# The state update in three split passes, the 31-tap convolution's sum in a PSUM bank, and three banks for small products

## The chip, the core and the metric

The kernel is one layer of a decoder trunk in fp32. It runs on one core of a Trainium2 chip: TensorE (PE) for matmuls, VectorE (DVE), ScalarE (ACT) and GpSimd (POOL) for everything else, SyncE (SP) for most transfers. The metric is the device time of one execution in microseconds (us), the median of several runs; lower is better.

## The reference

The layer mixes the positions of a sequence of 1024 rows with 1024 channels by two gated branches, projects the mix, and adds a gated feed-forward network with a small convolution. The parts that the change touches are the 31-tap convolution of the first branch and the chunked recurrence of the second:

```python
def conformer_branch(u_glu, dw_w, dw_b, ln_g, ln_b, w_out):
    a, g = jnp.split(u_glu, 2, axis=-1)
    v = a * jax.nn.sigmoid(g)
    v = causal_dwconv(v, dw_w, dw_b)             # 31 taps for each channel
    v = jax.nn.silu(layer_norm(v, ln_g, ln_b))
    return v @ w_out
# ssd_chunked, for chunks of 128 positions
    y_diag = jnp.einsum("bcgrls,bcsgrp->bclgrp", cb[:, :, :, None] * decay, xs)
    states = jnp.einsum("bclgn,bcgrl,bclgrp->bcgrpn", bc, decay_states, xs)
    # prev: the state carried into each chunk, decayed and added up
    y_off = jnp.einsum("bclgn,bcgrpn,bcgrl->bclgrp", cc, prev, jnp.exp(a_cs))
# the layer
    y_a = conformer_branch(u_glu, ...)
    y_b = ssd_branch(z, xbc, dt_raw, ...)
    mix = (jax.nn.sigmoid(gate_a) * y_a + jax.nn.sigmoid(gate_b) * y_b) @ w_o[l]
    h = layer_norm(DN_ALPHA * h + mix, ln1_g[l], ln1_b[l])
    h = layer_norm(DN_ALPHA * h + conv_ffn(h, ...), ln2_g[l], ln2_b[l])
```

## The kernel before

**Precision.** The large products keep fp32's accuracy by splitting each operand into a high part, rounded to the type fp32r, and a low part, the rest; `mm3` (L190 to L192) then makes three fp32r passes, high by high, high by low and low by high, in one accumulation. A weight block of 1024 rows and 128 columns is loaded, cast on ACT (L156), and its low part taken on DVE (L161); `project` runs eight such triples, 24 passes of 128x512, for one block of 128 output channels by 512 positions. Small products (transposes, the masks, the recurrence's own) are plain fp32 matmuls. In the profile one fp32 matmul shows as two instructions at L661, L808 and L820 (x56 there for 28 products).

**Stages.** The sequence is worked through in two halves of 512 positions (hh = 0, 1). For each half: `mixers`, then `combine`, then the output projection `out_proj` for hh = 0; the feed-forward part for both halves stands at the end, behind `mixers(1)` and `combine(1)`. In `mixers` four groups g follow each other. A group projects its columns (B, C, four of x, four of z, and two pairs for the convolution), convolves some with 4 taps (`conv4`, L517), gates the pairs (`glu`) into two tiles v, runs the recurrence (`ssd_group`) on four chunks of 128 positions, and the 31-tap convolution (`conv31`) on its two v. At the end come the first half of the recurrence branch's output projection and some gates.

**A chunk of the recurrence.** PE transposes four blocks of x into one PSUM bank (px, L614), and B of the chunk with the product of B and C into another (pb, L617 and L618). DVE makes xs and xsd from px (xs with the time step; xsd, L643, with the decay to the chunk's end), ACT copies the transposed B to bt, and DVE multiplies the decay mask m by the product (L648). Then PE forms the output py from m and xs (L653) and from the carried state and ce (L656), and the state's increment pn in one fp32 matmul of bt and xsd (L661). DVE decays the state (L665), adds pn (L668), and reads py in four skip additions (L671). `last` leaves the increment out in each group's last chunk of the second half: 28 increments in all.

**The 31-tap convolution.** For each v, ACT makes the first term with the bias in the accumulator c, and DVE adds thirty taps (L564, `scalar_tensor_tensor`, c = v shifted by k, times a column of weights, plus c). The two tiles of a group alternate, so each tap stands behind one of the other chain. Eight channel blocks c0_0 to c0_7 (c1_... in the second half), 480 taps in all. The sums of the first six blocks go to memory and come back later; the last two stay. The convolution has a low priority (offset -1500), so its taps fill DVE's gaps.

**Combine.** For the convolution branch's norm, POOL adds the eight blocks (L801, L803), PE takes the mean over channels with a matmul on a constant (L808, `deviations`), DVE subtracts it (L810), ACT squares (L812, L815), POOL adds the squares (L816, seven additions), PE takes the mean again (L820, `normed`), ACT the root (L821), DVE the reciprocal (L822), and for each block DVE multiplies (L825), ACT applies silu (L826), casts (L206), and DVE takes the low part (L207): that is sT, which the products with `wconv` (weights w_co) read. Around it PE has the products of the second gate (weights w_gb) and of the recurrence branch's second half (w_sp); DVE adds and multiplies their results into mb (L861, L862).

**Banks.** PSUM has eight banks: four (`pacc`, tiles acc) for the large products, and four (`psm`, tiles sm) through which all small products rotate.

**Order.** The program is recorded once; a scheduler, with priorities from the order of the code and the offsets given in it, lays the instructions out, engine by engine, and each engine works its own list strictly in that order. A tile that reuses a buffer waits for the readers of its former user.

Of the kernel before, what the change touches and what calls it, by code (L numbers as in the profile page):

```python
# [16 lines left out]
P = 128  # L17
# [6 lines left out]
KC = 31  # L24
# [37 lines left out]
def kernel(  # L62
# [28 lines left out]
    psm = ctx.enter_context(tc.tile_pool(name="psm", bufs=4, space=PSUM))  # L91
# [3 lines left out]
    def bank(which):  # L95
        n_ps[0] += 1
        pl, tag = (pacc, "acc") if which else (psm, "sm")
        return pl.tile([P, 512], F32, tag=tag, name=f"{tag}{n_ps[0]}")
# [187 lines left out]
    def ln_in_first():  # L286
        hT = big_tile("hT0")
        with pool("lnin0", side="right") as pl:
# [11 lines left out]
            for pair in range(2):  # L300
                with tc.high_priority(offset=3500 if pair else 6000):
                    pts = [bank(0).rearrange("p (k t) -> p k t", k=2) for _ in range(4)]
# [227 lines left out]
    def glu(pl, hh, hT, i):  # L530
        pa, pg = bank(1), bank(1)
        wa = col_weights(hh, CT_A + i)
        project(pa, wa, hT)
        wg = col_weights(hh, CT_G + i)
        project(pg, wg, hT)
        v = (statep if i & 2 else pl).tile(
            [P, HALF + KC - 1], F32, tag="v", bufs=2, name=f"v{hh}_{i}"
        )
        s = pl.tile([P, HALF], F32, tag="sig", name=f"sig{hh}_{i}")
        A.activation(out=s, in_=pg, func=AF.Sigmoid)  # L540
        A.copy(v[:, : KC - 1], v_halo[:, i, :])
        V.tensor_mul(v[:, KC - 1 :], pa, s)
        if hh == 0:
            A.copy(v_halo[:, i, :], v[:, HALF:])
        return v

    def conv31(pl, hh, vs):

        accs = {}
        for i, v in vs:  # L550
# [9 lines left out]
            accs[i] = c  # L560
        for k in range(KC - 1):
            for i, v in vs:
                wc = PC_CW + i * KC
                V.scalar_tensor_tensor(  # L564
                    out=accs[i],
                    in0=v[:, k : k + HALF],
                    scalar=pc[:, wc + k : wc + k + 1],
                    in1=accs[i],
# [3 lines left out]
        for i, _ in vs:  # L572
            if i < 6:
                SY.dma_start(c_scr[hh][i], accs[i])
# [15 lines left out]
    def ssd_group(pl, hh, g, xT, BT, CT, zs):  # L590
# [3 lines left out]
        def heads(t):  # L594
            return t.rearrange("p (h q) -> p h q", h=8)
# [5 lines left out]
        for c in range(4):  # L601
# [39 lines left out]
            if not last:  # L641
                xsd = pl.tile([P, HALF], F32, tag="xsd", name=f"xsd{nm}")
                V.tensor_tensor(  # L643
                    out=heads(xsd), in0=heads(px), in1=per_head(dts[1][:, c, h8]), op=ALU.mult
                )
                bt = pl.tile([P, P], F32, tag="bt", name=f"bt{nm}")
                A.copy(bt, pb[:, :P])
# [11 lines left out]
            if not last:  # L659
                pn = bank(0)  # L660
                TE.matmul(pn, bt, xsd, start=True, stop=True)  # L661
# [710 lines left out]
    state_stack.close()  # L1372
    ffn_stack = ExitStack()
# [121 lines left out]
```

## Time and profile before

| | |
|---|---|
| median of 3 runs | 1936.15 us (1934.88 to 1937.16) |
| span of the profiled execution | 1934.5 us |
| PE busy | 1921.9 us (99%) |
| DVE busy | 1600.7 us (83%) |
| ACT busy | 1092.2 us (56%) |
| POOL busy | 216.7 us (11%) |
| DMA | 376.27 MB, mean 195 GB/s |

The profile shows one execution. Its span is 1.65 us below the median of the runs. An engine's "busy" is the time in which it executes matmuls (PE), weight loads (PEld) or operations. Rows of a timeline give start, length, engine, line, operation, output and inputs by the program's names (buffer numbers left out), shape, count, and in brackets the idle time before and what ended it. Matmuls overlap in a pipeline, so the step from the start of one to that of the next says more than the length of either.

### The profile page before, as it was taken

What the parts mean: (1) busy time and instruction counts of PE and PEld (TensorE: products, weight loads), DVE (VectorE), ACT (ScalarE), POOL (GpSimd) and SP (SyncE); (2) the same over time, 40 slices, a digit from 0 to 9 for tenths busy, and PEclk for the clock granted to TensorE, in tenths of its full rate; (3) what the DMA queues carried; (4) which work ended last, traced back from release to release, by engine and by line L of the source; (5) the groups of instructions that cost most, each with busy time, mean ns of one, the idle gap of its engine ahead of it and who ended that gap; (6) DMA issues with size and microseconds to landing.
All of it is one profiled execution on the core that took longest, in us unless ns stands there. A gap on an engine that the chain in (4) does not pass through costs nothing.

```text
span 1934.5 us, 25807 instructions
## 1 busy us (share of the span) xinstructions
PE 1921.9 (99%) x9424; PEld 1570.4 (81%) x9424; DVE 1600.7 (83%) x2230; ACT 1092.2 (56%) x1641; POOL 216.7 (11%) x256
## 2 busy tenths in 40 slices
PE   9999999999999999999999999999999999999998
PEld 8888877788888788888888888888888888887886
DVE  7599999999897639899999546597788888888778
ACT  7576767753353366776765435365555555543544
POOL 1001010112300001111112140010000000122010
PEclk9999999999999999999999999999999999999999
DMA  6645555547456665656545644566455555479673
GB/s 231 219 169 200 172 201 185 167 160 267 135 183 228 207 208 176 211 177 211 177 162 166 219 143 135 182 241 225 163 171 185 178 185 185 161 276 355 198 250 115
DMA packets 127216, 376.27 MB, mean 195 GB/s; under 512 B 15184, under 2 KB 15728, under 8 KB 127088
## 3 DMA queue, kind: packets, MB, share of 16 engines
q1 hardware_dynamic: 107424, 318.48, 48.7%
q0 software_dynamic: 13184, 44.59, 6.5%
q10 hardware_dynamic: 6480, 11.55, 1.6%
q8 instruction: 74, 1.21, 0.3%
q14 instruction: 54, 0.44, 0.1%
HBM read 290.00 MB, written 84.56 MB: 194 GB/s over the span
## 4 chain that ended last, share of the span: by engine, by line
PE 86%; DVE 9%; DMA 3%; ACT 1%; issue 1%; SPq 0%; DVEq 0%; POOL 0%; ACTq 0%; POOLq 0%
PE acc L192 20%; PE acc L191 20%; PE acc L190 20%; PE sm L190 6%; PE sm L192 6%; PE sm L191 6%; DVE c L564 3%; DMA dr<-wdown 2%; PE sm L653 1%; PE sm L661 1%; PE sm L656 1%; DVE x L517 1%; PE acc L498 1%; DMA st_wo<-wo 1%; PE sm L614 1%
## 5 line engine op out<-in xcount | busy, mean ns | idle before, releaser
L192 PE MATMUL acc<-hT_h,w_c 128*128 128x512 f32 x1000 | 391.4, 392 | 0.0
L191 PE MATMUL acc<-hT_l,w_c 128*128 128x512 f32 x1000 | 391.1, 391 | 0.0
L190 PE MATMUL acc<-hT_h,w_c 128*128 128x512 f32 x1000 | 391.0, 391 | 0.0
L564 DVE SCALAR_TENSOR_TENSOR c<-v,pc,c 128x512 f32<-128x512 f32 x480 | 371.1, 798 | 7.0 <-ACT c L553 4.5
L190 PEld LDWEIGHTS acc<-hT_h,w_c 128*128 128x128 f32 x1000 | 187.8, 188 | 40.6 <-issue 1.9
L192 PEld LDWEIGHTS acc<-hT_h,w_c 128*128 128x128 f32 x1000 | 187.8, 188 | 40.4 <-issue 1.5
L191 PEld LDWEIGHTS acc<-hT_l,w_c 128*128 128x128 f32 x1000 | 187.8, 188 | 39.5 <-issue 1.1
L156 ACT CAST w_c<-st_c 128x1024 fp32r<-128x1024 f32 x128 | 133.8, 1046 | 111.4 <-PE acc L192 84.3
L632 POOL TENSOR_TENSOR ce<-ce,xbc 128x1024 f32<-128x1024 f32 x28 | 78.3, 2796 | 686.8 <-ACT ce L631 686.8
L1260 ACT CAST w_dn<-dr 128x1024 fp32r<-128x1024 f32 (+1 forms) x72 | 67.2, 942 | 76.7 <-DVE dr L1193 36.0
L190 PE MATMUL sm<-h1s,w_s 128*128 128x512 f32 x264 | 102.8, 389 | 0.5 <-ACT fuv L1103 0.5
L191 PE MATMUL sm<-h1s,w_s 128*128 128x512 f32 x264 | 102.7, 389 | 0.0
L192 PE MATMUL sm<-h1s,w_s 128*128 128x512 f32 x264 | 102.2, 389 | 0.0
L621 ACT ACTIVATE m<-ab,acs 128x128 f32<-128x128 f32 x256 | 78.4, 390 | 39.5 <-PE sm L653 37.8
L161 DVE TENSOR_TENSOR w_c<-st_c,w_c 128x1024 fp32r<-128x1024 f32 x62 | 76.7, 1237 | 17.5 <-ACT w_c L156 17.4
L1261 DVE TENSOR_TENSOR w_dn<-dr,w_dn 128x1024 fp32r<-128x1024 f32 (+1 forms) x72 | 77.6, 1084 | 6.3 <-ACT w_dn L1260 6.2
L517 DVE SCALAR_TENSOR_TENSOR x<-u,pc,x 128x512 f32<-128x512 f32 x96 | 78.0, 826 | 5.7 <-ACT x L515 5.6
L192 PE MATMUL acc<-h1b_h,w_ue 128*128 128x512 f32 x176 | 68.7, 395 | 0.3 <-DVE w_ue L161 0.3
L190 PE MATMUL acc<-h1b_h,w_ue 128*128 128x512 f32 x176 | 68.8, 391 | 0.0
L191 PE MATMUL acc<-h1b_l,w_ue 128*128 128x512 f32 x176 | 68.6, 390 | 0.0
L190 PE MATMUL sm<-h1b_h,w_s 128*128 128x512 f32 x176 | 68.5, 389 | 0.0
L191 PE MATMUL sm<-h1b_l,w_s 128*128 128x512 f32 x176 | 68.5, 389 | 0.0
(369 smaller groups left out, 4544.7 us busy)
## 6 DMA issues: line engine op xcount, KB each, us to landing
st_c<-wcol SPq DMA_DIRECT2D x128, 512.0 KB, 4.4
low_scr<-w_c SPq DMA_DIRECT2D x64, 512.0 KB, 2.9
w_c<-low_scr SPq DMA_DIRECT2D x64, 512.0 KB, 4.4
ab<-acs_scr SPq DMA_DIRECT2D x32, 512.0 KB, 4.2
dr<-wdown SPq DMA_DIRECT2D x55, 256.0 KB, 4.9
st_wo<-wo SPq DMA_DIRECT2D x24, 512.0 KB, 4.3
st_ue<-wup SPq DMA_DIRECT2D x22, 512.0 KB, 3.7
first_scr<-first ACTq DMA_DIRECT2D x44, 256.0 KB, 3.0
```

Source lines behind the costliest of these rows:

```text
L156: casts.append(A.copy(w[:, 0, :], st))
L161: sub.tensor_tensor(out=w[:, 1, :], in0=st, in1=w[:, 0, :].bitcast(F32), op=ALU.subtract)
L190: TE.matmul(ps, wa(0), xa(0), start=start, stop=False, skip_group_check=more)
L191: TE.matmul(ps, wa(0), xa(1), start=False, stop=False, skip_group_check=more)
L192: TE.matmul(ps, wa(1), xa(0), start=False, stop=stop, skip_group_check=more)
L498: mm = TE.matmul(pss[o][:, ts], ws[o][:, i, k * P : (k + 1) * P], hT[:, j, k, ts], start=n == 0 and k == 0, stop=n == 2 and k == KD - 1,)
L517: V.scalar_tensor_tensor(out=o, in0=u[:, k : k + HALF], scalar=pc[:, wc + k : wc + k + 1], in1=o, op0=ALU.mult, op1=ALU.add,)
L564: V.scalar_tensor_tensor(out=accs[i], in0=v[:, k : k + HALF], scalar=pc[:, wc + k : wc + k + 1], in1=accs[i], op0=ALU.mult, op1=ALU.add,)
L621: A.activation(out=m[:, h, :], in_=ab[:, h, :], func=AF.Relu, scale=-1.0, bias=acs[:, c, 8 * g + h : 8 * g + h + 1],)
L632: G.tensor_tensor(out=ce, in0=ce, in1=CT[:, cs].unsqueeze(1).to_broadcast([P, 8, P]), op=ALU.mult)
L1260: A.copy(w[:, 0, cs], src)
L1261: V.tensor_tensor(out=w[:, 1, cs], in0=src, in1=w[:, 0, cs].bitcast(F32), op=ALU.subtract)
```

## The change

The state's increment pn becomes a three-pass product: bt and xsd become pairs of high and low parts (ACT casts, DVE subtracts; xsd is first formed whole in a tile of its own), and `mm3` replaces the single matmul. In `conv31` the two chains no longer alternate: each tile's thirty taps follow one another, the running sum lies in a PSUM bank of its own (pool `pconv`, one buffer), the first tap reads c and the last writes c. The bank comes from the small products: `psm` has three in `mixers` and `combine`, and four again for the feed-forward part, after both pools are closed. At the kernel's head, `pconv`'s bank serves as the fourth transpose tile. The tile of `glu`'s sigmoid moves to another tag.

```diff
-    psm = ctx.enter_context(tc.tile_pool(name="psm", bufs=4, space=PSUM))
+    mixers_psum = ExitStack()
+    psm = [mixers_psum.enter_context(pool("psm", 3, space=PSUM))]
+    pconv = mixers_psum.enter_context(pool("pconv", 1, space=PSUM))
...
-        pl, tag = (pacc, "acc") if which else (psm, "sm")
+        pl, tag = (pacc, "acc") if which else (psm[-1], "sm")
...
-                    pts = [bank(0).rearrange("p (k t) -> p k t", k=2) for _ in range(4)]
+                    pts = [bank(0) for _ in range(3)]
+                    pts.append(pconv.tile([P, 512], F32, tag="conv", name=f"head{pair}"))
+                    pts = [pt.rearrange("p (k t) -> p k t", k=2) for pt in pts]
...
-        s = pl.tile([P, HALF], F32, tag="sig", name=f"sig{hh}_{i}")
+        s = pl.tile([P, HALF], F32, tag="ya", bufs=2, name=f"sig{hh}_{i}")
...
-            accs[i] = c
-        for k in range(KC - 1):
-            for i, v in vs:
-                wc = PC_CW + i * KC
+            acc = pconv.tile([P, HALF], F32, tag="conv", name=f"conv{hh}_{i}")
+            for k in range(KC - 1):
                 V.scalar_tensor_tensor(
-                    out=accs[i],
+                    out=acc if k < KC - 2 else c,
                     in0=v[:, k : k + HALF],
                     scalar=pc[:, wc + k : wc + k + 1],
-                    in1=accs[i],
+                    in1=acc if k else c,
                     op0=ALU.mult,
                     op1=ALU.add,
                 )
-        for i, _ in vs:
+            accs[i] = c
             if i < 6:
-                SY.dma_start(c_scr[hh][i], accs[i])
+                SY.dma_start(c_scr[hh][i], c)
...
-                xsd = pl.tile([P, HALF], F32, tag="xsd", name=f"xsd{nm}")
+                xsd = pl.tile([P, 2, HALF], F32R, tag="xsd", name=f"xsd{nm}")
+                whole = pl.tile([P, HALF], F32, tag="whole", name=f"whole{nm}")
                 V.tensor_tensor(
-                    out=heads(xsd), in0=heads(px), in1=per_head(dts[1][:, c, h8]), op=ALU.mult
-                )
-                bt = pl.tile([P, P], F32, tag="bt", name=f"bt{nm}")
-                A.copy(bt, pb[:, :P])
+                    out=heads(whole), in0=heads(px), in1=per_head(dts[1][:, c, h8]), op=ALU.mult
+                )
+                bt = pl.tile([P, 2, P], F32R, tag="bt", name=f"bt{nm}")
+                for n, src in ((bt, pb[:, :P]), (xsd, whole)):
+                    A.copy(n[:, 0, :], src)
+                    V.tensor_tensor(
+                        out=n[:, 1, :], in0=src, in1=n[:, 0, :].bitcast(F32), op=ALU.subtract
+                    )
...
                 pn = bank(0)
-                TE.matmul(pn, bt, xsd, start=True, stop=True)
+                mm3(pn, lambda i: bt[:, i, :], lambda i: xsd[:, i, :], True, True)
...
     state_stack.close()
+    mixers_psum.close()
+    psm.append(ctx.enter_context(pool("psm4", 4, space=PSUM)))
```

The scheduler lays the instructions out anew. Up to the end of `mixers(1)` every engine's list changes; behind it the lists are the same, instruction by instruction. Lines move too: the passes of `mm3` are L192 to L194 in the changed kernel, the taps L566, py L660 and L663, the mean and variance matmuls L815 and L827, the deviations L817, the variance's additions on POOL L823.

The first place is PE's list at the state increment of the first group's second chunk (sm35 is pn before, sm33 in the changed kernel; x4 and xbc are the next chunk's x and B, C; acc a large product). Before:

```order
L653 MATMUL sm34_1173<-m0_0_1_1151,xs0_0_1_1166 64x128 x2
L656 MATMUL sm34_1173<-ce0_0_1_1161,state0_105 64x128 x2
L661 MATMUL sm35_1190<-xsd0_0_1_1168,bt0_0_1_1170 128x512
L614 MATMUL sm36_1205<-ident_75,x4_0_0_695 128x128 x4
L617 MATMUL sm37_1210<-ident_75,xbc0_16_676 128x128
L618 MATMUL sm37_1210<-xbc0_20_686,xbc0_16_676 128x128
L191 MATMUL acc48_1556<-hT0_l_310,w_c0_22_1559 128x512
```

And in the changed kernel:

```order
L660 MATMUL sm32_1186<-m0_0_1_1160,xs0_0_1_1175 64x128 x2
L663 MATMUL sm32_1186<-ce0_0_1_1170,state0_108 64x128 x2
L192 MATMUL sm33_1203<-xsd0_0_1_1177,bt0_0_1_1180 128x512
L193 MATMUL sm33_1203<-xsd0_0_1_1177,bt0_0_1_1180 128x512
L194 MATMUL sm33_1203<-xsd0_0_1_1177,bt0_0_1_1180 128x512
L616 MATMUL sm34_1220<-ident_78,x4_0_0_698 128x128 x4
L194 MATMUL acc46_1585<-hT0_h_312,w_c0_22_1588 128x512
```

One matmul has become three, and the transpose of B with the product of B and C no longer follows the transposes of x at once: it stands behind passes of a large product, and takes a bank that py of the chunk before has held.

The second place is PE's list around the norm of the convolution branch in the first half (sm161 and sm166 are the mean's and the variance's bank before, sm159 and sm164 in the changed kernel; stats0 holds the two sums). Before, the first matmul of the mean stands behind block w_sp0_2, and the second, 96 passes on, behind w_sp0_4:

```order
L192 MATMUL acc160_4669<-yT0_2_h_4079,w_sp0_2_4672 128x512
L808 MATMUL sm161_4701<-stats0_4445,mean_w_93 128x512
L190 MATMUL acc162_4726<-hT0_h_309,w_gb0_4_4729 128x512
L192 MATMUL acc165_4826<-yT0_2_h_4079,w_sp0_4_4829 128x512
L820 MATMUL sm166_4858<-stats0_4445,mean_w_93 128x512
L190 MATMUL acc167_4895<-hT0_h_309,w_gb0_6_4898 128x512
```

In the changed kernel the mean's matmul stands behind the first three passes of w_sp0_7, the last block before w_co; the variance's follows behind the block's other 21 passes:

```order
L194 MATMUL acc169_5136<-yT0_2_h_4184,w_sp0_7_5139 128x512
L815 MATMUL sm159_4808<-stats0_4552,mean_w_96 128x512
L192 MATMUL acc169_5136<-yT0_2_h_4184,w_sp0_7_5139 128x512
L827 MATMUL sm164_4965<-stats0_4552,mean_w_96 128x512
L192 MATMUL acc170_5172<-sT0_4969,w_co0_0_5175 128x512
L192 MATMUL acc171_5208<-sT0_4969,w_co0_1_5211 128x512
L192 MATMUL acc172_5244<-sT0_4969,w_co0_2_5247 128x512
L193 MATMUL acc170_5172<-sT0_4969,w_co0_0_5175 128x512
```

Before, 120 passes of w_gb and w_sp stand between the variance's matmul and the first product that reads sT; in the changed kernel none do, and three blocks of w_co are worked side by side. In the second half the distances stay nearly as they were.

The third place is DVE's list at the same point (c0_7 is the last block's sum in SBUF, conv0_7 its running sum in PSUM; sp and gb name the weights' low parts). Before:

```order
L564 SCALAR_TENSOR_TENSOR c0_7_4208<-v0_7_3557,pc_99,c0_7_4208 128x512 x3
L861 TENSOR_TENSOR mb0_1_4513<-yb0_1_4601,acc158_4603 128x512
L862 TENSOR_TENSOR mb0_1_4513<-mb0_1_4513,gb0_1_4508 128x512
L161 TENSOR_TENSOR w_gb0_4_4729<-st_gb0_4_4727,w_gb0_4_4729 128x1024
L161 TENSOR_TENSOR w_sp0_3_4763<-st_sp0_3_4761,w_sp0_3_4763 128x1024
L861 TENSOR_TENSOR mb0_2_4514<-yb0_2_4667,acc160_4669 128x512
L862 TENSOR_TENSOR mb0_2_4514<-mb0_2_4514,gb0_2_4599 128x512
L810 TENSOR_TENSOR cc0_0_4521<-cc0_0_4521,sm161_4701 128x512 x2
```

And in the changed kernel:

```order
L868 TENSOR_TENSOR mb0_5_4624<-yb0_5_5034,acc166_5036 128x512
L566 SCALAR_TENSOR_TENSOR conv0_7_4346<-v0_7_3638,pc_102,conv0_7_4346 128x512
L869 TENSOR_TENSOR mb0_5_4624<-mb0_5_4624,gb0_5_4929 128x512
L163 TENSOR_TENSOR w_sp0_7_5139<-st_sp0_7_5137,w_sp0_7_5139 128x1024
L566 SCALAR_TENSOR_TENSOR conv0_7_4346<-v0_7_3638,pc_102,conv0_7_4346 128x512 x2
L566 SCALAR_TENSOR_TENSOR c0_7_4344<-v0_7_3638,pc_102,conv0_7_4346 128x512
L163 TENSOR_TENSOR w_co0_0_5175<-st_co0_0_5173,w_co0_0_5175 128x1024
L868 TENSOR_TENSOR mb0_6_4625<-yb0_6_5100,acc168_5102 128x512
L869 TENSOR_TENSOR mb0_6_4625<-mb0_6_4625,gb0_6_5032 128x512
L163 TENSOR_TENSOR w_co0_1_5211<-st_co0_1_5209,w_co0_1_5211 128x1024
L817 TENSOR_TENSOR cc0_0_4628<-cc0_0_4628,sm159_4808 128x512 x2
```

The last tap and the deviations stand four blocks of w_sp later than before: from mb0_1 to mb0_5, and from mb0_2 to mb0_6.

## Prediction

> **What bounds the kernel now.** I read first the profile's page: busy shares of the engines, and the chain that ended last.
>
> ```profile
> PE 1921.9 (99%) x9424; PEld 1570.4 (81%) x9424; DVE 1600.7 (83%) x2230; ACT 1092.2 (56%) x1641; POOL 216.7 (11%) x256
> PE 86%; DVE 9%; DMA 3%; ACT 1%; issue 1%; SPq 0%; DVEq 0%; POOL 0%; ACTq 0%; POOLq 0%
> ```
>
> PE is the bound: in a span of 1934.5 us it is idle for 12.6. So a change gains where it shortens PE's own work, and loses where it makes PE wait. Next the busy time by stretches: the middle of the first half's mixers, the two stretches around the norm of the convolution branch, and the rest.
>
> ```profile
> 120.00:490.00 370.00, 370.00 (x1976) 297.65 (x1975) 367.59 (x540) 240.39 (x402) 46.49 (x31) 1.00 0.55 190
> 510.40:533.00 22.60, 22.60 (x99) 18.38 (x98) 14.79 (x16) 9.89 (x14) 11.68 (x8) 1.00 0.45 158
> 533.10:561.00 27.90, 27.90 (x123) 22.77 (x122) 24.18 (x32) 23.46 (x30) 2.12 (x4) 1.00 0.51 176
> 561.00:1080.00 519.00, 518.40 (x2745) 421.54 (x2744) 441.14 (x689) 310.48 (x495) 51.77 (x26) 1.00 0.57 193
> 1080.00:1930.00 850.00, 844.27 (x3740) 693.69 (x3738) 648.63 (x790) 423.74 (x553) 92.65 (x170) 1.00 0.58 198
> ```
>
> The columns are window, length, then busy us of PE, PEld, DVE, ACT and POOL. Two things carry the forecast. In the mixers DVE is as full as PE (367.6 of 370 us): the convolution's taps, of low priority, fill every gap it has, so any DVE work added there pushes the last tap back by as much. And between the norm's two mean matmuls, and from the second to the first use of its result, PE has 22.6 and 27.9 us of other work: those two stretches hide a long chain over DVE, ACT and POOL.
>
> **The state product.** The timeline's rows of PE, then the group of the old product.
>
> ```profile
> 126.16 1.13 PE L661 MATMUL sm<-xsd,bt 128*128 128x512 f32 x2
> 127.12 0.60 PE L614 MATMUL sm<-ident,x 128*128 128x128 f32 x4
> 163.61 0.39 PE L192 MATMUL acc<-hT_h,w_c 128*128 128x512 f32 x1
> 163.83 0.39 PE L190 MATMUL acc<-hT_h,w_c 128*128 128x512 f32 x1
> 164.15 0.33 PE L653 MATMUL sm<-m,xs 128*64 128x128 f32 x2
> L661 PE MATMUL sm<-xsd,bt x56: 592/645/697, 108.1 to 1057.4; 128*128 128x512 f32 x56
> ```
>
> The old product is recorded as two matmuls, 56 for the 28 products, and the next work starts 127.12 - 126.16 = 0.96 us after it. A split pass of the same size takes 163.83 - 163.61 = 0.22 us (0.227 on the mean of a run of them), three take 0.68. That is 28 x 0.28 = 7.9 us less for PE. Against it: from a split pass to a full-precision matmul the step is 164.15 - 163.83 = 0.32, 0.09 more than between two passes; if each of the 28 products pays that once, 2.5 us go, so the gain lies between 5.4 and 7.9. I take 7, nearer the upper end, because the scheduler can set passes beside passes.
>
> The splitting adds per product one cast of 128x512 on ACT (the copy of bt becomes a cast of the same size), and on DVE a subtract of 128x512 that reads SBUF and one of 128x128 that reads PSUM. Their nearest rows follow, with those for the taps.
>
> ```profile
> 545.95 0.60 ACT L206 CAST sT<-cc 128x512 fp32r<-128x512 f32 x1
> 546.59 0.69 DVE L207 TENSOR_TENSOR sT<-cc,sT 128x512 fp32r<-128x512 f32 x1 [0.86 <-ACT sT L206]
> L643 DVE TENSOR_TENSOR xsd<-sm,wds x28: 673/676/682, 98.1 to 1045.6; 128x512 f32<-128x512 f32 x28
> L564 DVE SCALAR_TENSOR_TENSOR c<-v,pc,c x480: 653/741/2897, 90.3 to 1079.0; 128x512 f32<-128x512 f32 x160
> 497.51 3.10 DVE L564 SCALAR_TENSOR_TENSOR c<-v,pc,c 128x512 f32<-128x512 f32 x4
> 165.42 1.40 DVE L564 SCALAR_TENSOR_TENSOR c<-v,pc,c 128x512 f32<-128x512 f32 x2
> 166.75 0.68 DVE L665 TENSOR_TENSOR state<-state,edc 128x512 f32<-128x512 f32 x1
> ```
>
> The big subtract is 0.69 with about 0.6 from start to start, the small one a third of that: 0.8 us for each product, 28 x 0.8 = 22 us of DVE, 11 in each half. ACT gets 28 x 0.60 = 17 us and is 240.39 of 370 us busy in the mixers; that hides.
>
> **The convolution.** The number of taps stays 480. A pair on two accumulators takes 166.75 - 165.42 = 1.33 us, 0.67 a tap; four on one accumulator in a row take 3.10, 0.76 to 0.78 a tap. In the changed order 219 taps stand directly behind a tap of the same chain, 70 before: 149 x 0.1 = 15 us more DVE, if a tap that adds into PSUM costs what it costs in SBUF. From below: the PSUM-reading 128x512 operations (L643, 0.676) are as short as the shortest taps and never stretched, while the taps reach 2.9 us; their median of 0.741 would fall by 0.06, 480 x 0.06 = 29 us less. From above: unknown, no row adds from PSUM into PSUM on DVE; I take as far end 1.0 us for a dependent tap, as a rival below. My value is about even, so DVE's load rises by some 22 us in all, all in the mixers.
>
> Since DVE is full there, this comes out at the end of each half: in the first half 11 us late. The changed kernel's order says the same more strongly: the last tap of c0_7 stands behind mb0_5, where it stood ahead of mb0_1, and the deviations stand behind mb0_6 instead of mb0_2.
>
> **The norm of the convolution branch, first half.** This is the largest term. The chain before, from the timeline:
>
> ```profile
> 504.13 1.30 POOL L803 TENSOR_TENSOR stats<-stats,c 128x512 f32<-128x512 f32 x1 [10.09 <-DVE c L564]
> 510.38 1.02 PE L808 MATMUL sm<-stats,mean_w 128*128 128x512 f32 x2
> 511.91 2.47 DVE L810 TENSOR_TENSOR cc<-cc,sm 128x512 f32<-128x512 f32 x4
> 512.63 0.63 ACT L812 ACTIVATE stats<-cc 128x512 f32<-128x512 f32 x1 [0.95 <-DVE cc L810]
> 513.93 11.59 POOL L816 TENSOR_TENSOR stats<-stats,csq 128x512 f32<-128x512 f32 x7 [8.51 <-ACT csq L815]
> L816 POOL TENSOR_TENSOR stats<-stats,csq x14: 1292/1303/2160, 513.9 to 1149.6; 128x512 f32<-128x512 f32 x14
> 533.02 1.02 PE L820 MATMUL sm<-stats,mean_w 128*128 128x512 f32 x2
> 534.28 1.28 ACT L821 ACT_TABLE_LOAD   x1
> 535.58 0.69 ACT L821 ACTIVATE stats<-sm,eps 128x512 f32<-128x512 f32 x1
> 536.30 3.35 DVE L822 RECIPROCAL stats<-stats 128x512 f32<-128x512 f32 x1 [0.53 <-ACT stats L821]
> 539.69 3.70 DVE L825 TENSOR_TENSOR cc<-cc,stats 128x512 f32<-128x512 f32 x6
> 543.82 2.23 ACT L826 ACTIVATE cc<-cc,pc 128x512 f32<-128x512 f32 x3
> 561.09 0.39 PE L190 MATMUL acc<-sT,w_co 128*128 128x512 f32 x1
> ```
>
> Call X the start of the first mean matmul. The variance's sum is ready at 513.93 + 11.59 = 525.5, X + 15.1; with seven additions at the median, 7 x 1.303 = 9.1, it is X + 12.6. Before, PE had 22.6 us of other work there. In the changed order the mean matmul stands three passes into the last weight block, w_sp0_7, and the second mean matmul follows after the other 21: 1.0 + 21 x 0.227 = 5.7 us. Nothing else stands between, and PE takes its work in order. So PE idles 6.9 to 9.4 us.
>
> Behind the second mean matmul come directly the products with w_co0, which read sT. From its start to the first part of sT: matmul and start of the root about 1.3 (533.02 to 534.28, with the table not counted), root 0.69, reciprocal 3.35, first multiplication 0.7, first silu 0.75, cast 0.60, with the hand-overs about 8.0; PE has 1.0 of it to do, so it idles 7.0, when the tables are loaded in time. Then the eight casts and low parts come one by one: cast, silu and subtract at about 1.4 us of ACT for each of 8, against nine passes (2.0 us) that the three blocks do for each part. The first low part stands behind all eight multiplications (0.6 each), 10.9 us after the start: another 2.2 of waiting. Together 6.9 to 9.4, plus 7.0, plus 2.2: 16.1 to 18.6, and I take 17.5. The mean itself should not be late: its last addition needs c0_7's last tap and 1.30 of POOL, and DVE has that tap some 7 us before X (it stands behind mb0_5, whose product ends two blocks of 5.4 us earlier).
>
> In the second half the distances between these matmuls are kept, and everything behind the mixers stands as it did: nothing there.
>
> **The clock.** At the start of the kernel PE, busy all the time, finishes half as many matmuls in a window at first:
>
> ```profile
> 2.00:4.00 2.00, 2.00 (x11) 2.00 (x10) 0.04 (x1) 1.97 (x4) 0.45 (x2) 1.00 0.88 309
> 4.00:6.00 2.00, 2.00 (x12) 2.00 (x11) 1.50 (x4) 0.18 (x1) 0.00 (x0) 1.00 1.03 418
> 6.00:8.00 2.00, 2.00 (x20) 2.00 (x20) 2.00 (x6) 0.87 (x3) 0.00 (x0) 1.00 1.03 422
> ```
>
> Eleven and twelve against twenty, while the granted clock reads 1.00. If an idle of 7 us brings that back, each of two idles costs up to 2 us (some 4 us at about half rate): 0 to 4, taken 1.5, because part of the slow time lies where PE waits anyway. The Trainium skill ("TensorE: Matmul & The Clock Gate", section "What's actually happening") says the array falls to half its clock after an idle window of some 3.4 us and returns after as long a busy one; by it the two idles would cost about 1.7 us each, an estimate of 3.4, and the sum would be 1.9 higher than mine.
>
> **Three banks.** The small products rotate through three banks, so the bank of a chunk's products B and C now comes free only when the skip additions on DVE have read the py of the chunk before. PE reaches that place after 25 to 42 passes, in most chunks, 5.7 to 9.5 us. Two chunks of before, one early and the worst:
>
> ```profile
> 165.73 0.39 PE L656 MATMUL sm<-ce,state 128*64 128x128 f32 x4
> 167.35 1.11 DVE L671 SCALAR_TENSOR_TENSOR x<-x,pc,sm 128x128 f32<-128x128 f32 x4
> 949.34 0.39 PE L656 MATMUL sm<-ce,state 128*64 128x128 f32 x4
> 955.50 1.11 DVE L671 SCALAR_TENSOR_TENSOR x<-x,pc,sm 128x128 f32<-128x128 f32 x4
> ```
>
> From the end of the last product with the state to the end of the skip additions it is 168.46 - 166.12 = 2.3 us in the one and 956.61 - 949.73 = 6.9 in the other, against 5.7 to 9.5 of cover: most chunks keep a margin of 1.5 to 4 us, a few have none. I take 0.5 us, between 0 and 13: with 2 us more lag the nine or so chunks with the least margin wait about 1.5 each.
>
> **The sum**: -7 + 17.5 + 1.5 + 0.5 = +12.5 us. On the profiled span of 1934.5 that is 1947.0. The runs' median, 1936.15, is 1.65 above the span: 1948.5 (rounded).
>
> **Rivals.** (A, faster.) PE's stall is taken back: while it waits, DVE, ACT and the loads get ahead, and waits that PE had later go. Only what PE waits later can be given back: 0.6 us from 561 to 1080 and 5.7 from 1080 to 1930, by the windows. For a faster kernel the stall must also shrink below 7, which the seven additions on POOL (9.1 us against 5.7 of cover) and the 8 us from root to sT forbid unless the order on PE is not what runs. If the stall vanished the time would be 1936.15 - 7 = 1929. Chance 5%.
>
> (B) DVE becomes the bound. If a tap that adds into PSUM behind another costs 1.0 us rather than 0.77, 219 x 0.23 = 50 us more DVE, 25 in each half. Before the mean is late there are 5.8 us to spare (the 7 less 1.3 on POOL); the rest, about 19, shows in PE at the first mean matmul, and as much in the second half where DVE's lead over PE is smaller: 1948.5 + 20 to 38, about 1970 to 1985. For it: DVE is full. Against it: L643 reads PSUM and is no longer than a tap. The Trainium skill ("VectorE: DVE Perf Modes", section "The TRN2 errata") gives a PSUM source 120 cycles of fixed cost against 58 for SBUF at 0.96 GHz; as an estimate that is 0.065 us on each of 464 taps that read PSUM, 30 us more DVE, and a time of about 1960. The trace's rows disagree: 0.676 with a PSUM operand, 0.68 (L665) without. Chance 8% for DVE.
>
> (C) The waits for three banks are real in all chunks, because DVE's skip additions are pushed back by taps that stand ahead of them: 1 us of lag costs about 5 us, 2 us about 13, on top of the sum: 1953 to 1961. Chance 10%.
>
> (D) The stall is half of what I think, because the tail of sT's parts overlaps with PE better and the mean is early: 1940 to 1944, and about even at the far end. 6% for slower by over 0.2%, 4% for even.
>
> **How the numbers follow.** My forecast has 67%, A 5, B 8, C 10, D 10. The likeliest case has its own range: from -7.9 + 16.1 + 0 + 0 = +8.2 to -5.4 + 18.6 + 4 + 3 = +20.2, that is 1944 to 1956. The range reaches into D and C, down to 1941 and up to 1959, and leaves out A, B and the ends of C and D. About 0.2% (4 us) is what a measurement of this kernel can tell from no change; faster by more than that has 5%, within it 4%, slower by more 91%.
>
> **What would show it.** In the changed profile: three passes of about 0.23 at L192 to L194 in place of L661; taps of L566 at 0.65 to 0.78; a PE idle of 7 to 9 us ahead of L827, released by POOL L823, and one of about 7 ahead of the first w_co0 product, released by ACT or DVE on sT; hardly any idle at L619. I am wrong if PE's total idle stays near 13 us, if the idle lies ahead of L815 (the mean late: B), or if it lies in many small pieces at L619 (C).

## The result, and the profile after

The changed kernel takes 1958.47 us, the median of 4 runs (1955.28 to 1959.17), against 1935.92 for the kernel before: 1.0111 of its time, 95% interval 1.0098 to 1.0124. That is 22.5 us slower, where 12.5 were forecast. The profiled execution has a span of 1956.8 us, 22.3 longer than before. From the page, the busy times and two rows of slices (40 of 48.9 us each):

```profile
PE 1924.7 (98%) x9452; PEld 1577.1 (81%) x9452; DVE 1621.3 (83%) x2286; ACT 1107.8 (57%) x1670; POOL 204.9 (10%) x256
PE   9999999999969999999999999999999999999998
PEclk9999999999979999999999999999999999999999
```

PE is now idle for 1956.8 - 1924.7 = 32.1 us instead of 12.6, and one slice holds most of the difference: the twelfth, 538 to 587 us, where the granted clock dips too. PE's waits, by what ended them (total us, times, longest):

```profile
PE sm L827 <- POOL stats L823: 8.8, 1, 8.8
PE acc L192 <- ACT sT L208: 7.0, 1, 7.0
PE acc L193 <- DVE sT L209: 1.1, 1, 1.1
```

All three are new, and all are in the norm of the convolution branch in the first half; no other new wait is longer than 1.1 us in all. The timeline of PE there:

```profile
555.02 1.02 PE L815 MATMUL sm<-stats,mean_w 128*128 128x512 f32 x2
569.63 2.08 PE L827 MATMUL sm<-stats,mean_w 128*128 128x512 f32 x2 [8.82 <-POOL stats L823]
578.66 1.65 PE L192 MATMUL acc<-sT,w_co 128*128 128x512 f32 x3 [6.95 <-ACT sT L208]
582.00 0.63 PE L194 MATMUL acc<-sT,w_co 128*128 128x512 f32 x1
582.43 0.63 PE L192 MATMUL acc<-sT,w_co 128*128 128x512 f32 x1
586.27 0.51 PE L192 MATMUL acc<-sT,w_co 128*128 128x512 f32 x1
```

Before, PE went from the mean's matmul to the first product with w_co without a wait. Now it stops twice. Behind the second stop each pass takes 582.43 - 582.00 = 0.43 us, up to 586.27, then 0.23 again. The same stretch by windows (window, length, busy us of PE, PEld, DVE, ACT, POOL, then the granted clock):

```profile
561.00:569.00 8.00, 0.00 (x0) 0.00 (x0) 4.78 (x5) 4.63 (x6) 7.61 (x6) 0.82 0.29 98
569.00:578.60 9.60, 2.08 (x2) 0.50 (x2) 6.10 (x6) 3.99 (x6) 1.13 (x2) 0.50 0.16 55
578.60:586.20 7.60, 6.44 (x14) 4.63 (x15) 5.91 (x10) 7.60 (x14) 1.58 (x3) 0.50 0.40 140
586.60:594.20 7.60, 7.60 (x35) 6.27 (x34) 7.22 (x13) 1.87 (x4) 0.46 (x1) 1.00 0.40 131
```

Fourteen passes in 7.6 us at a clock of 0.50, then 35 in the same time at 1.00. The clock had fallen before that: in windows of 1 us it reads 1.00 up to 566 us, some 5 us into the first stop, and 0.50 from there to 586, so also during the second stop.

The starts of the same instructions on PE show where in the program the 22.3 us stand (us):

| start on PE | before | after | difference |
|---|---|---|---|
| py of the first chunk | 107.11 | 109.04 | 1.9 |
| first w_gb block, first half | 472.29 | 472.73 | 0.4 |
| first w_sp block, first half | 483.17 | 483.61 | 0.4 |
| first w_co block, first half | 561.09 | 578.66 | 17.6 |
| output projection, first half | 606.28 | 629.41 | 23.1 |
| first w_gb block, second half | 1108.91 | 1129.56 | 20.7 |
| end of the last matmul | 1926.88 | 1949.08 | 22.2 |

So the stretch from the first half's w_sp blocks to its output projection costs 22.7 us and the kernel's head 1.9; the first half's mixers give 1.5 back, the output projection and the second half's mixers 2.5, and what follows loses 1.5 again.

### The profile page after: what moved, and what is told of

Same layout as the page of the kernel before. It is cut to its first block, busy times and chain, and to the rows that moved or that the text cites. A ratio compares the mean times of both kernels' runs of the same rounds, so it can differ in the third digit from the quotient of the medians.

```text
span 1956.8 us, 25962 instructions
## 1 busy us (share of the span) xinstructions
PE 1924.7 (98%) x9452; PEld 1577.1 (81%) x9452; DVE 1621.3 (83%) x2286; ACT 1107.8 (57%) x1670; POOL 204.9 (10%) x256
## 4 chain that ended last, share of the span: by engine, by line
PE 80%; DVE 12%; ACT 3%; DMA 3%; issue 2%; POOL 1%; SPq 0%; DVEq 0%; ACTq 0%; POOLq 0%
PE acc L194 19%; PE acc L193 19%; PE acc L192 19%; PE sm L192 6%; PE sm L194 6%; PE sm L193 6%; DVE conv L566 3%; DMA dr<-wdown 1%; PE sm L660 1%; DVE x L521 1%; PE sm L663 1%; PE acc L502 1%; DMA st_wo<-wo 1%; DVE w_c L163 1%; DVE c L1200 1%
## 5 line engine op out<-in xcount | busy, mean ns | idle before, releaser
L192 PE MATMUL acc<-hT_h,w_c 128*128 128x512 f32 x1000 | 392.1, 392 | 0.4 <-ACT zs L583 0.4
L194 PE MATMUL acc<-hT_h,w_c 128*128 128x512 f32 x1000 | 391.1, 391 | 0.0
L566 DVE SCALAR_TENSOR_TENSOR conv<-v,pc,conv 128x512 f32<-128x512 f32 x448 | 336.2, 750 | 7.4
L192 PEld LDWEIGHTS acc<-hT_h,w_c 128*128 128x128 f32 x1000 | 187.8, 188 | 40.9 <-ACT u L518 0.8
L194 PEld LDWEIGHTS acc<-hT_h,w_c 128*128 128x128 f32 x1000 | 187.8, 188 | 38.7 <-issue 0.2
L634 POOL TENSOR_TENSOR ce<-ce,xbc 128x1024 f32<-128x1024 f32 x28 | 69.2, 2472 | 695.1 <-ACT ce L633 695.1
L192 PE MATMUL sm<-h1s,w_s 128*128 128x512 f32 x264 | 102.8, 389 | 0.5 <-ACT fuv L1110 0.5
L194 PE MATMUL sm<-h1s,w_s 128*128 128x512 f32 x264 | 102.2, 389 | 0.0
L521 DVE SCALAR_TENSOR_TENSOR x<-u,pc,x 128x512 f32<-128x512 f32 x96 | 72.2, 766 | 8.1 <-ACT x L519 8.1
L192 PE MATMUL acc<-h1b_h,w_ue 128*128 128x512 f32 x176 | 68.7, 391 | 0.0
L194 PE MATMUL acc<-h1b_h,w_ue 128*128 128x512 f32 x176 | 68.5, 394 | 0.0
L192 PE MATMUL sm<-h1b_h,w_s 128*128 128x512 f32 x176 | 68.5, 389 | 0.0
```

Of the source, the lines that this page charges most:

```text
L192: TE.matmul(ps, wa(0), xa(0), start=start, stop=False, skip_group_check=more)
L194: TE.matmul(ps, wa(1), xa(0), start=False, stop=stop, skip_group_check=more)
L521: V.scalar_tensor_tensor(out=o, in0=u[:, k : k + HALF], scalar=pc[:, wc + k : wc + k + 1], in1=o, op0=ALU.mult, op1=ALU.add,)
L566: V.scalar_tensor_tensor(out=acc if k < KC - 2 else c, in0=v[:, k : k + HALF], scalar=pc[:, wc + k : wc + k + 1], in1=acc if k else c, op0 ...
L634: G.tensor_tensor(out=ce, in0=ce, in1=CT[:, cs].unsqueeze(1).to_broadcast([P, 8, P]), op=ALU.mult)
```

## The experiments

Each ratio is the time divided by that of the kernel before on the same chip, with its 95% interval. Profiles show one execution of several; it lies up to 3 us from the median unless the text says otherwise. The diffs are cut (...).

**The split product alone.** The kernel before with this part of the diff (and the sigmoid's tile on the other tag):

```diff
+                bt = pl.tile([P, 2, P], F32R, tag="bt", name=f"bt{nm}")
+                for n, src in ((bt, pb[:, :P]), (xsd, whole)):
...
-                TE.matmul(pn, bt, xsd, start=True, stop=True)
+                mm3(pn, lambda i: bt[:, i, :], lambda i: xsd[:, i, :], True, True)
```

> The kernel before with the split state product alone (and the sigmoid's tile on the other tag): four banks, the convolution in SBUF with two chains. Its order has 73 passes between the mean's and the variance's matmul of the first half and 48 between the variance's and the first w_co product. Theory (the loss is the norm's chain in the first half, because its last tap is laid too late, and PE itself works less): 73 passes are 16.5 us against a chain of 12.6 to 15.1, and 48 are 10.9 against 8.0, so no idle there; the product saves about 5 us: 1931, between 1929 and 1934. Rival (DVE's 22 us of added work are the cause, since DVE is as full as PE in the mixers): PE waits for m or xsd in the chunks, 1940 or more.

Measured: 1944.61 us against 1937.10, 1.0044 (1.0031 to 1.0058). My theory missed and the rival came out. PE's waits, in an execution of 1950.86, the slowest of the six:

```profile
PE sm L658 <- DVE m L653: 5.2, 5, 1.7
PE sm L813 <- POOL stats L808: 2.1, 1, 2.1
PE acc L191 <- DVE sT L207: 2.1, 1, 2.1
PE acc L192 <- DVE w_sp L161: 1.6, 1, 1.6
```

The split's work on DVE costs in two places. PE waits 5.2 us for the mask m, all of it in the second half's mixers. And from the first w_sp block to the output projection PE loses 12.5 us. The three other waits are 5.8 of it: for the low part of a weight block, for the last tap's sum ahead of the mean's matmul, and for a low part of sT. (The two covers that I had counted, up to the variance's matmul and up to sT's first part, held.) Behind the two waits of 2.1 us, six or seven passes run at 0.43 us, at a granted clock of 0.50 to 0.53, before the step falls back to 0.23. So a loss at the norm exists without the PSUM sum too. Its size in the median execution is not shown: that one is 6.2 us shorter than the one profiled. No run has the sigmoid's other tile alone, so its share is not shown either.

**The convolution in PSUM and three banks, without the split.** The changed kernel with the old product:

```diff
...
-                mm3(pn, lambda i: bt[:, i, :], lambda i: xsd[:, i, :], True, True)
+                TE.matmul(pn, bt, xsd, start=True, stop=True)
```

> The changed kernel with the state product in one fp32 matmul as before: convolution in PSUM one chain after the other, three banks. Its order has 76 passes between the two matmuls of the norm and 48 behind. Theory: the chain is covered, so the time is that of before plus what the head of the kernel loses (about 2 us by the landmarks): 1937 to 1939. Rival (taps into PSUM slower, or three banks make PE wait): 1945 or more, with PE idle ahead of the products of B and C.

Measured: 1941.02, 1.0022 (1.0013 to 1.0031): 2 to 4 us above what I expected and 4 below the rival. The profiled execution is 2.6 us longer than the one before: it loses 1.5 at the head and 4.4 between the first w_co product and the output projection, where PE waits once for a low part of sT (2.1 us), and gets the rest back elsewhere. No wait for a bank shows. Behind this wait of 2.1 us the passes stay at 0.23 and the clock at 1.00.

**Three banks alone.** The kernel before with this:

```diff
-    psm = ctx.enter_context(tc.tile_pool(name="psm", bufs=4, space=PSUM))
+    psm = [mixers_psum.enter_context(pool("psm", 3, space=PSUM))]
...
```

> The kernel before with three banks for small products, the fourth used only as the head's fourth transpose tile; convolution and state product as before. Order of the norm as before (96 and 120 passes). Theory: 1936 to 1938 (0 to 2 for the head). Rival (three banks cost PE waits in all chunks): 1941 to 1949.

**All but the sum in PSUM.** The changed kernel with:

```diff
...
-                    out=acc if k < KC - 2 else c,
+                    out=c,
...
-                    in1=acc if k else c,
+                    in1=c,
```

> The changed kernel with the running sum of the convolution in SBUF (the tile c) instead of the PSUM bank, the chains still one after the other; the split product and three banks stay. Its order has the norm as before: 96 passes and 120. Theory (the place of the last tap in the order makes the loss, and taps cost the same in both memories): 1931 to 1935. Rival (DVE's load, or dependent taps one behind another, make the loss): within 5 of the changed kernel, 1953 to 1960.

Measured: 1958.33, 1.0114 (1.0101 to 1.0127), for three banks alone, and 1962.80, 1.0134 (1.0121 to 1.0147), for all but the sum in PSUM. I missed both by more than 20 us, and both rivals' ranges as well. Their norms are covered as expected; they lose in the mixers. Waits of PE, with three banks alone:

```profile
PE acc L192 <- ACT zs L585: 9.3, 2, 5.9
PE sm L622 <- DVE x L675: 1.3, 1, 1.3
PE sm L621 <- DVE x L675: 0.9, 1, 0.9
```

and with all but the sum in PSUM:

```profile
PE acc L192 <- ACT zs L582: 7.7, 3, 3.5
PE sm L618 <- DVE x L677: 4.5, 2, 2.3
```

The rows that end in "DVE x" are the wait of my rival C: the bank of B and C's products comes free with the skip additions. In their orders PE has only 10 and 14 passes of large products (three banks alone) or none (the other) between py and that place at the last chunk of the second and third groups, where the changed kernel has 24 and 23. At those places PE then runs out of large products, because their accumulators wait for ACT:

```profile
357.20 0.39 PE L622 MATMUL sm<-xbc,xbc 128*128 128x128 f32 x2
363.53 0.79 PE L192 MATMUL acc<-hT_h,w_c 128*128 128x512 f32 x1 [5.94 <-ACT zs L585]
```

So three banks do cost, in some orders: these two kernels are 16 and 24 us late at the end of the first half's mixers, some 2 of it from the head; the changed kernel escapes that. Both of these have the taps in SBUF; why the order with the sum in PSUM keeps more passes there was not settled by a run.

**Filling PE's idle time.** The changed kernel with 36 and 30 passes whose results nobody reads, in the two stops; every list is otherwise as it was:

```diff
...
+            def filler(spare):
+                mm = TE.matmul(spare, hT[:, 0, 0, :P], hT[:, 0, 0, :], start=True, stop=True)
...
+                issue_after(fillers[0], sp_mms[-1])
+                issue_after(var_mm[0], fillers[-1])
```

> The changed kernel, every list as it is, with passes of 128x512 added on PE whose results nobody reads: 36 between the last pass of w_sp0_7 and the variance's matmul, 30 between that and the first w_co product. They are 8.2 and 6.8 us and so fit in the two idle stretches of 8.8 and 7.0. Theory of the clock (the slow passes at 0.427 us behind the idle are TensorE at half rate, brought on by the idle): the passes behind run at 0.227, some 18 of them, and the variance's matmul in 1.0 instead of 1.9: 4 us less, about 1954. Rival (those passes are slow because sT arrives part by part): no change, 1957 to 1960.

Measured: 1953.76, 1.0085 (1.0071 to 1.0098). The theory's 1954. The timeline and the window at the place of the slow passes:

```profile
578.03 0.97 PE L193 MATMUL acc<-sT,w_co 128*128 128x512 f32 x3
580.78 0.50 PE L194 MATMUL acc<-sT,w_co 128*128 128x512 f32 x1 [1.79 <-DVE sT L213]
578.00:586.20 8.20, 6.38 (x27) 4.98 (x28) 5.92 (x10) 8.18 (x14) 1.86 (x4) 1.00 0.45 141
```

The clock stays at 1.00 and the passes at 0.23, so the slow passes came with PE's idle time. Useless work makes the kernel 4.7 us faster by the medians, 3.5 by the two profiled executions. Only 1.8 of that lies between the first w_sp block and the output projection (144.0 us instead of 145.8): the start on w_co is just 0.6 us earlier, since sT sets it, and the faster passes then wait longer, 2.6 us in three places instead of 1.1. Another 1.8 lie behind the second half's first w_gb block, where the traces of all these kernels spread from 816 to 821 us. The Trainium skill ("TensorE: Matmul & The Clock Gate", section "What's actually happening") gives half the clock until some 3.4 us of busy time have passed. The half rate agrees; the length agrees in the run with the split alone (slow passes from 569.57 to 572.56 behind one wait, of only 2.1 us), not here, where they run from 578.66 to 586.27 with another wait of 1.1 inside, 4.9 us of it without a break.

**Less work on DVE ahead of the last tap.** The changed kernel with the low parts of the first half's w_gb blocks on POOL, then with those of five w_c blocks too:

```diff
-                project(pg, weights(wcol[CT_GB + j], f"gb{hh}_{j}"), hT)
+                project(pg, weights(wcol[CT_GB + j], f"gb{hh}_{j}", sub=V if hh else G), hT)
...
-            project(pg, col_weights(hh, CT_GA + j), hT)
+            project(pg, col_weights(hh, CT_GA + j, V if hh or j < 3 else G), hT)
```

> The changed kernel with the low parts of the eight w_gb blocks of the first half made on POOL instead of DVE: eight subtracts of 1.2 us less for DVE ahead of the last tap. Its order has 76 passes (17.2 us) between the two matmuls of the norm, none between the second and w_co. Theory (DVE's load ahead of the last tap sets the norm's place, the norm's chain sets the loss): the first idle (8.8 and 0.8 of slow matmul) goes, the second stays: about 1949. Rival (the loss moves elsewhere with DVE's load, or POOL's traffic slows DVE by as much): 1956 to 1962.

> As the run before, with the low parts of five w_c blocks for the first gate on POOL too. Its order has 75 passes between the two matmuls and 29 (6.6 us) behind the second. Theory: both idles go but 1 to 2 us, and with them the slow clock: about 1940. Rival: 1954 to 1962.

Measured: 1947.85, 1.0052 (1.0038 to 1.0065), and 1945.90, 1.0044 (1.0032 to 1.0057). The first is as expected: the stop at the variance's matmul is gone, the one at w_co stays. The second should have been at 1940. PE at the norm in that run:

```profile
554.33 1.02 PE L827 MATMUL sm<-stats,mean_w 128*128 128x512 f32 x2
567.12 1.65 PE L192 MATMUL acc<-sT,w_co 128*128 128x512 f32 x3 [5.18 <-ACT sT L208]
569.54 0.63 PE L194 MATMUL acc<-sT,w_co 128*128 128x512 f32 x1
```

From the variance's matmul to sT it takes 12.8 us, not the 9.0 of the changed kernel, because DVE and ACT have other work between the steps (casts and low parts of w_co among it). 6.6 us of passes were meant to cover it; the stop is 5.2 long, and the half clock comes with it.

**Fewer taps.** The changed kernel without 36 taps of the first half's last two blocks:

```diff
-            for k in range(KC - 1):
+            for k in range(18 if hh == 0 and i > 5 else 0, KC - 1):
```

> The changed kernel without the first 18 of the 30 taps of the two last channel blocks of the first half (36 taps of 0.75 us, 27 us of DVE; the output lacks them). Its order has the norm nearly where it was before: 95 passes and 120 behind. Theory: no idle at the norm, 1958.5 less 21: 1937, and 1 less where the mixers' end gets easier. Rival (three banks or the split cost PE time in the mixers as they did in the variants with the sum in SBUF): 1945 or more.

Measured: 1938.75, 1.0010 (1.0002 to 1.0019). The first py, the first w_gb block and the first w_sp block of the first half start on PE within 0.1 us of where they do in the changed kernel. The norm has no stop:

```profile
511.05 1.02 PE L815 MATMUL sm<-stats,mean_w 128*128 128x512 f32 x2
533.47 1.02 PE L827 MATMUL sm<-stats,mean_w 128*128 128x512 f32 x2
```

With 27 us of DVE taken away, some 20 of the 22.5 us of loss go. The rest of the change as a whole is about even (1.9 us slower).

**POOL takes the splitting.** The split product in the kernel before, then in the changed kernel, with xsd's subtract on POOL (and low parts of weights as above):

```diff
-                    V.tensor_tensor(
+                    (G if n is xsd else V).tensor_tensor(
                         out=n[:, 1, :], in0=src, in1=n[:, 0, :].bitcast(F32), op=ALU.subtract
```

> The state product split as in the change, but four banks and the convolution as before; the 128x512 subtract of each product (xsd's low part) and the low parts of the first half's eight w_gb blocks are on POOL. DVE then gets 0.2 us a product instead of 0.8, and the order has the norm exactly where it was before (96 and 120 passes). Theory (the split saves PE some 5 us when DVE isn't loaded for it): 1931 to 1934, and none of the 5 us of waits for the mask m that the run with the split alone shows in the second half. Rival (POOL's additional traffic stretches DVE's two-input operations by as much as it takes off them): 1938 or more.

> The changed kernel whole, with xsd's low parts, the first half's w_gb low parts and those of five w_c blocks on POOL. Its order has 85 passes (19 us) between the norm's two matmuls and over 70 behind the second. Theory (the norm's chain is all that the changed kernel loses beyond the head): no idle at the norm, 1936 to 1939, as without the 36 taps. Rival: 1943 or more, PE waiting somewhere in the mixers.

Measured: 1965.38, 1.0148 (1.0135 to 1.0161), and 1948.45, 1.0062 (1.0049 to 1.0075). Both rivals came out. In the first of the two, PE's waits and the taps' group:

```profile
PE acc L192 <- DVE w_sp L161: 7.5, 2, 4.4
PE sm L658 <- DVE m L653: 6.0, 5, 2.5
L564 DVE SCALAR_TENSOR_TENSOR c<-v,pc,c x480: 644/740/4467, 90.8 to 1113.1; 128x512 f32<-128x512 f32 x160
```

Taps with two inputs in SBUF are stretched while POOL works, here up to 4.5 us (2.9 before): in both traces, every stretched tap of the mixers overlaps an operation of POOL. In 110 to 470 us a tap takes 0.868 us on average, 0.794 before, and PE waits for what DVE makes. Here the remedy is worse than the load that it removes: the split alone took 1944.61. In the second, the norm has no stop, as the theory said, but PE waits 5.6 us for the mask m in the two halves' mixers. It is 10 us faster than the changed kernel, and no faster than the two kernels with low parts of weights alone on POOL.

**The passes alone.** The kernel before with three passes in place of the product, without low parts:

```diff
-                TE.matmul(pn, bt, xsd, start=True, stop=True)
+                for _ in range(3):
+                    TE.matmul(pn, bt, xsd, start=True, stop=True)
```

> The kernel before with three split-type passes in place of the one fp32 product, and nothing else: xsd and bt are written as high parts by the operations that wrote them before, the three passes all take the high parts and overwrite each other, so the low parts are left out of the state. DVE, ACT and POOL do what they did. Theory (the passes save PE 5 us and only DVE's splitting takes it back): 1931 to 1933. Rival (PE gains nothing because what it waits for follows it): 1935 to 1937.

Measured: 1936.60 against 1936.60, 1.0003 (0.9994 to 1.0012). No gain that can be measured; the rival came out. In the profiled execution (1934.17) the first half's mixers are 2.6 us shorter on PE, 0.16 for each of their 16 products; the head is 0.8 longer, and part of the rest goes into waits.

None of the kernels tried is faster than the one before.

## Why the prediction was right, and where its sizes were off

The direction, the mechanism and the range (1941 to 1959) held, at the range's upper edge; the sum of +12.5 was 10 us short. That the time lies in the range is partly luck: the forecast's own terms gave 1944 to 1956, and the range went up to 1959 for rival C, which did not come. By the trace, the missing 10 us are some 4 at the norm with the clock, 3 of the state product's gain, 2 at the head, and 1.5 behind the second half's first w_gb block, which is within what executions differ by there.

**The norm, first half** (16.1 to 18.6, taken 17.5, and 1.5 for the clock). Right in mechanism, term by term. The steps behind PE's two stops:

```profile
548.23 0.75 DVE L566 SCALAR_TENSOR_TENSOR c<-v,pc,conv 128x512 f32<-128x512 f32 x1
549.12 1.30 POOL L810 TENSOR_TENSOR stats<-stats,c 128x512 f32<-128x512 f32 x1 [36.76 <-DVE c L566]
559.02 10.55 POOL L823 TENSOR_TENSOR stats<-stats,csq 128x512 f32<-128x512 f32 x7 [8.60 <-ACT csq L822]
571.74 0.69 ACT L828 ACTIVATE stats<-sm,eps 128x512 f32<-128x512 f32 x1 [2.88 <-PE sm L827]
572.46 3.35 DVE L829 RECIPROCAL stats<-stats 128x512 f32<-128x512 f32 x1 [6.68 <-ACT stats L828]
```

X is 555.02. The last tap ends at 548.98, 6 us ahead (forecast 7), so the mean is not late. The variance's sum is ready at 569.57, X + 14.6 (12.6 to 15.1); the first stop is 8.8 (6.9 to 9.4). From there to sT it is 9.0 us (8.0), with a stop of 7.0 (7.0), and the low parts add 1.1 (2.2). The three stops make 16.9. What was too small is the clock: 1.5 taken, between 0 and 4. At 0.50 of the clock the variance's matmul takes 2.08 instead of 1.02, and the passes from 578.66 to 586.27 lose 3.3, so 4.4 in all; filling the stops won less than that at the norm, because PE then waited more for sT. About 1 more are eight transposes of the next stage that the new order puts there (24 instead of 16), which I had not counted. The whole norm measured 22.7 instead of 19.0.

**The state product** (-7, between -5.4 and -7.9). This step failed. One product of the changed kernel:

```profile
128.66 0.50 PE L192 MATMUL sm<-xsd,bt 128*128 128x512 f32 x1
128.99 0.39 PE L193 MATMUL sm<-xsd,bt 128*128 128x512 f32 x1
129.22 0.40 PE L194 MATMUL sm<-xsd,bt 128*128 128x512 f32 x1
129.46 0.60 PE L616 MATMUL sm<-ident,x 128*128 128x128 f32 x4
```

It takes 0.80 us, not 0.68: the first pass behind a short full-precision matmul costs 0.33. The 0.96 for the old one holds, in 24 of 28 places as the step to the next start. In the other four a split pass follows 0.56 us after the product, and is itself held up, to 0.63 instead of 0.23, so that the two together cost the same:

```profile
166.05 1.12 PE L661 MATMUL sm<-xsd,bt 128*128 128x512 f32 x2
166.61 0.80 PE L191 MATMUL acc<-hT_l,w_c 128*128 128x512 f32 x1
167.24 0.39 PE L192 MATMUL acc<-hT_h,w_c 128*128 128x512 f32 x1
```

So the gain is 0.16 us a product, 4.5 in all. The sum had put the cost of switching behind the passes; it is paid at the first. The mixers of the changed kernel gave back 1.5 us in the first half and, with the output projection, 2.5 in the second: 4.0 where 7 were taken. And the split's work on DVE costs more than that elsewhere, as the runs with the split alone (+7.5) and with the passes alone (even) show.

**What was left out.** The head: the first py starts 1.5 to 2.4 us later in every kernel whose fourth transpose tile is the convolution's bank, and 0.1 to 0.8 later in the three without it. I had given it nothing. No run has this tile alone.

**The convolution.** "About even" was right where DVE's time is concerned. The taps' groups of the changed kernel, into PSUM from PSUM and from SBUF:

```profile
L566 DVE SCALAR_TENSOR_TENSOR conv<-v,pc,conv x448: 672/751/757, 93.0 to 1112.2; 128x512 f32<-128x512 f32 x150
L566 DVE SCALAR_TENSOR_TENSOR conv<-v,pc,c x16: 746/760/1306, 92.2 to 1078.4; 128x512 f32<-128x512 f32 x16
```

A tap into PSUM behind another takes 0.75, not the 1.0 of my rival, and is never stretched (757 ns at most, 2897 before); the sixteen first taps, with both inputs in SBUF, still reach 1306. Four in a row took 3.12 us, in SBUF 3.10. The 65 ns more for a PSUM source that the Trainium skill's table ("VectorE: DVE Perf Modes", section "The TRN2 errata") gives do not show. But the last tap came 45 us later, not 11. The windows' rows of all engines, then of the taps alone, before:

```profile
0.00:505.00 505.00, 503.26 (x2700) 409.44 (x2701) 467.18 (x700) 322.89 (x547) 58.10 (x48) 1.00 0.56 194
0.00:505.00 505.00, 186.87 (x240) 1.00 0.56 194
```

and changed, with the group of the split's larger subtract:

```profile
0.00:505.00 505.00, 501.43 (x2714) 411.94 (x2715) 453.91 (x698) 330.64 (x561) 52.01 (x46) 1.00 0.56 195
0.00:505.00 505.00, 153.15 (x205) 1.00 0.56 195
505.00:549.00 44.00, 27.49 (x36) 1.00 0.35 119
L652 DVE TENSOR_TENSOR xsd<-whole,xsd 128x512 fp32r<-128x512 f32 x16 | 10.9, 684 | 2.9 <-ACT xsd L651 2.9
```

At 505 us 35 taps more are left, 27.5 us of DVE, and they stand between the w_gb and w_sp blocks' own work. The order showed the place rightly; the 11 us that I gave as its reason are only part of it. First, 16 of the 28 products stand in the first half, so half of the split's work was too little: its two subtracts are 10.9 and 4.5 us busy there. Second, DVE is not busier for it, as I had assumed, but works 13.3 us less up to 505 us (453.9 instead of 467.2). So DVE spends 33.7 us less on taps there: 20.4 went to its other work and 13.3 to waits. The waits lie in many places, such as 2.9 us ahead of xsd's subtract, for ACT's cast; why the new order has them was not settled by a run.

**Three banks** (0.5). Right for this kernel: no wait for pb among PE's waits. As a rule it would have been wrong: the same three banks with the sum in SBUF cost 21 us.

**Rivals.** A needed the stop taken back later; what came back behind the norm is 2.5 us by the second half's w_gb. B's price for a tap was wrong, but its mechanism, PE waiting for a full DVE, is what the split alone shows. C's range, 1953 to 1961, holds the measured time, but not for C's reason. D is out.

## What to carry to other kernels

Where a second engine is as full as the one that bounds the kernel, work added to it, and time that it loses to waits, come out at the end of the stage, here in the first chain that the bound engine must wait for: find that place in the new order, count what the bound engine still has to do between the chain's steps, and price the chain by the rows of before. Price a new instruction sequence by its whole run, with the steps into and out of it and the delay of what stands behind. Where a scheduler lays out the program anew, the parts of a change do not add up: here the split alone cost 7.5 us, the sum in PSUM with three banks 3.9, three banks alone 21, and all of it 22.5.

## What the runs showed of the hardware

- TensorE's granted clock fell to 0.50 some 5 us into an idle stretch of 9 us, stayed there through a second one of 7 us, and was back 7.6 us after work had begun again. Behind two waits of 2.1 us in another kernel, passes were slow for 3 to 4 us; behind one as long in a third kernel they were not. Passes without use in the long stretches kept the clock at 1.00 and made the kernel 4.7 us faster by the medians, 1.8 of it at the norm by the trace.
- A full-precision matmul delays the first split pass behind it: to the next start it is 0.33 us behind a short one and 0.63 behind one of 128x512, instead of 0.23.
- A dependent tap on DVE costs the same into PSUM as into SBUF (0.75 to 0.78 us), and only the one with both inputs in SBUF is stretched while POOL works: up to 4.5 us for one.
